# Weight-block sums made in DRAM ahead of time, scan fill redistributed, and operand halves loaded into other tiles, in a hybrid SSM and attention layer

## The chip, the cores and the metric

One Trainium2 chip, one of its cores. The metric is the device time of one execution in microseconds (us); lower is better. Engines: TensorE (PE; PEld is its weight load), VectorE (DVE), ScalarE (ACT), GpSimd (POOL), SyncE (SP). SP and ACT issue plain DMAs, POOL issues DMAs that may add to what lies at their destination.

## The reference

One layer, 512 tokens, width 2048, all in float32:

```python
h = rmsnorm(x, norm_w)
u = h @ w_in
z_ssm, xbc, dt_f, dt_b, q_a, kv_a, z_attn, g_ssm, g_attn = jnp.split(u, cuts, axis=-1)
xbc = jax.nn.silu(dwconv(xbc, conv_w, conv_b))
xs, bm, cm = jnp.split(xbc, ...)          # 32 heads of 64, 4 groups, state 128
y = ssd_scan(forward) + flip(ssd_scan(flipped)) + d_skip * xs       # chunks of 128 tokens
y = rmsnorm(y * silu(z_ssm), by group) * ssm_norm_w
q = rmsnorm(q_a) @ w_uq;  kv = rmsnorm(kv_a) @ w_ukv                # 16 heads, rotary part of 64
o = bidir_attention(q, k, v) * jax.nn.silu(z_attn)
merged = sigmoid(g_ssm) * (y @ w_proj_ssm) + sigmoid(g_attn) * (o @ w_proj_attn)
return rmsnorm(x + merged @ w_out, final_norm_w)
```

## The kernel before

**Arithmetic.** Each float32 operand is split in two parts: `h` is its copy rounded to TensorE's float32r format, made on ScalarE, and `l` the rest, made on VectorE. A product is three matmuls (h·h, h·l, l·h) of 512 columns into PSUM. A weight chunk is 128 x 1024 floats (512 KB): loaded by SP into one of three `wraw` buffers (or into `X` or `Y`, below), split into `wh` and `wl` (three buffers each), and used by 24 matmuls in the projections of the input, 12 in the blocked products.

**Order of work.** TensorE's instructions run in the order in which the program emits them. The other engines' are put in order by a scheduler with priorities: `tc.high_priority(offset=n)` lets an instruction pass n others, and `keep_in_program_order` pins one. Weight loads have an offset of 160 (`LOAD_AHEAD`), splits 60 (`AHEAD`). A tile pool recycles its buffers by tag; a pool that opens over the memory of a closed one waits tile by tile for the last users there.

**Stages.** (1) RMSNorm of x, transposed into `h_h`, `h_l`; the first input columns (`xbc_gen`, group 0); sums of blocks of h for the next stage (`h_sums`); `S3` and `x21` are stored in DRAM. (2) Three gates (`wz`, `wgs`, `wga`), each a 2048 x 2048 weight multiplied by Strassen-Winograd with seven block products per half (`Strassen.pair`, `cp` 0 and 1): P1, P5, P6, P2, P3, P7, P4, each 48 matmuls. Ahead of them S3 is loaded back and split over `x21` in `h_h`/`h_l`; P7 uses it. (3) The bidirectional scan, four groups (`ssd_group`). A group begins with transposes, goes through the states of its chunks (the state phase), and then makes the decay matrices and diagonal parts chunk by chunk (`seg_make`, `diag`: the chunk phase, VectorE's scans). Between these steps `gap()` emits a share of the fill: the generators of the remaining input columns (`xbc`, `qkv`, `za`), 10 tiles of 48 matmuls per group, in 18 gaps of equal share. `y_norm` normalises y, `y_turn` transposes it on TensorE and stores it in `yn_d`. (4) Preparation of attention (`compressed`, rotary tables), with the rest of the fill. (5) Attention, 16 heads: `scores`, `trans`, `pv`, with the heads' own weights as fill, and at its end `wps.head()` (P1 and P2 of both halves of the y projection). (6) The two projections, `wps` (y) and `wpa` (o): `wps.pair(0, True)`, `wps.pair(1, True)` (P5, P6, P3, P7, P4), `wpa.pair(0)`, `wpa.pair(1)` (all seven). (7) The output product, residual and last norm.

**Block sums of weights.** P5 and P6 need sums of weight blocks, P7 another. In `pair`, with the blocks named by row half and column half, `X` is loaded with block (0,0), and POOL's accumulating DMA (`w_more`) adds block (0,1) to it in SBUF; P5 uses X and adds `Y`, block (1,1), to it on VectorE for P6; (1,0) is added for P4. `Y` is used by P3, then `w_more` adds (0,1) to it for P7. `X` and `Y` have four buffers each. `y_ops` and `o_ops` hold the sums of operand blocks: made in DRAM by POOL (`sums`), loaded in halves by `raw_load` into `wraw`, split by `Ops.split` into slots of tag `opb` (five) or `opa`. The hooks of `wps` and `wpa` say behind which product a load (`L`), a split (`C`) or a part of the sums of o (`o_sums`) is emitted.

**Between attention and the projections** the pool `at` closes and `xb` opens on its memory; S1 and S2 of y are loaded and split, S4 is loaded, and `fill.all()` emits what is left of the head.

**PSUM banks** of a product come from a table by the product's name (`SETS`); the transposes of merged results use the banks of the product before the last.

Of the kernel before, what the change touches and what calls it, by code (L numbers as in the profile page):

```python
# [18 lines left out]
P = 128  # L19
# [53 lines left out]
def build(tc, a):  # L73
# [50 lines left out]

    OPS = ("x11", "x12", "x21", "x22", "S1", "S2", "S3", "S4")
# [206 lines left out]
    class Fill:  # L332
# [16 lines left out]
        def run(self, n):  # L349
            while n > 0 and self.q:  # L350
                n -= self.step()
# [108 lines left out]

    def w_more(t, w, cp, kh, cb, m, ahead_=AHEAD):

        with tc.high_priority(offset=ahead_):
            pool.dma_start(t, a[w][cp, kh, cb, m], accum_op=ALU.add)
# [41 lines left out]
    before_ = deque(["P1", "P1"])  # L506

    def turn_bank(i):

        return SETS[before_[0]][i]("turn")  # L510

    def product(name, op, chunk, extra=None, pre=None):

        bs = [b(name) for b in SETS[name]]
# [16 lines left out]
        before_.append(name)  # L531
        before_.popleft()
# [3 lines left out]
    class Strassen:  # L536
# [47 lines left out]
        def pair(self, cp, headed=False):  # L584
            w = self.w
            X, Y = [], []
            if not headed:
                def c1(m):
                    X.append(w_load(w_tile("X"), w, cp, 0, 0, m))
                    return X[m]  # L590

                p1 = evict((yield from product("P1", self.op("x11"), c1, lambda m, raw: w_more(raw, w, cp, 0, 1, m))), "p1")
# [33 lines left out]
            B = yield from product("P3", self.op("S4"), lambda m: Y[m], lambda m, raw: w_more(raw, w, cp, 0, 1, m),  # L626
# [6 lines left out]
            A = yield from product("P7", self.op("S3"), lambda m: Y[m], None, self.pre(2, 2 * cp + 1))  # L633
# [61 lines left out]
    h_ops.load("S3")  # L695
    for q in range(2):
        h_part("S3", 256, q)
# [19 lines left out]
    def h_back():  # L717
        h_ops.raws["x21"] = []
        for q in range(2):
# [5 lines left out]
                                      ("wga", h_ops, 1, gate(AF.Sigmoid, ga_d)))]  # L725
    gates[2].hooks = {(1, "P7"): [h_back, lambda: [h_part("x21", 256, q) for q in range(2)]]}
# [56 lines left out]
    def y_norm(c, g, y):  # L783
# [7 lines left out]
        dve.tensor_scalar_mul(y, y, rsqrt1(s_))  # L791
# [15 lines left out]
    def ssd_group(g):  # L807
# [727 lines left out]
```

## Time and profile before

| | |
|---|---|
| time, median of 3 runs | 2138.2 us (2128.6 to 2139.95) |
| the profiled execution | 2139.41 us, its span 2137.6 us, mean TensorE clock 0.966 |
| TensorE busy | 1982.9 us (93%), 9074 matmuls |
| VectorE, ScalarE, GpSimd busy | 1469.5 us (69%), 953.0 us (45%), 259.0 us (12%) |
| DMA | 349.20 MB, mean 163 GB/s |

```profile
## 2 busy tenths in 40 slices
PE   6989999999998998997999799999984989999998
PEld 5878888888776777786787688888873767877886
DVE  7966677677569679798687566767662878776342
ACT  5444444444535445445445344444442435444232
POOL 0001010100032221331221000000001010000110
PEclk9999999999999999998999899999996999999999
DMA  5457656855635535565444843524559788876332
```

Each digit is a slice of 53 us and the busy share in tenths. The gates lie in slices 3 to 11, the scan in 11 to 22, attention in 24 to 31, the projections in 31 to 37. A row of the lists has line, engine, operation, written tile <- read tiles, shape, count, then busy us, mean ns of one and idle time ahead of it with what ended most of it. A row of waits has the total in us, the number, and the longest. "Idle ... <-" in a timeline row stands in square brackets.

### The profile page before, as it was taken

Reading aid. Unit: us, or ns where it says so; the run is one execution under the profiler, and the core shown is the slowest. Engines: PE = TensorE matmul, PEld = TensorE weight load, DVE = VectorE, ACT = ScalarE, POOL = GpSimd, SP = SyncE. Lnnn points to the kernel's source line nnn. Section 1 sums busy time; section 2 is a strip of 40 time slices with the busy share of each in tenths; the row PEclk is TensorE's granted clock in tenths of the full one; section 3 lists DMA queues with packets and bytes.
Section 4 is the critical chain, followed back from the end, with each engine's and each line's share of the span. In section 5 each row is a group of like instructions: output and inputs, shape, how many; then the busy total and the mean of one; then the engine's idle time right before and its main releaser. Section 6 shows DMA issues by size and latency. Waiting matters only on the chain.

```text
span 2137.6 us, 24587 instructions
## 1 busy us (share of the span) xinstructions
PE 1982.9 (93%) x9074; PEld 1635.5 (77%) x9074; DVE 1469.5 (69%) x1962; ACT 953.0 (45%) x1332; POOL 259.0 (12%) x225
## 2 busy tenths in 40 slices
PE   6989999999998998997999799999984989999998
PEld 5878888888776777786787688888873767877886
DVE  7966677677569679798687566767662878776342
ACT  5444444444535445445445344444442435444232
POOL 0001010100032221331221000000001010000110
PEclk9999999999999999998999899999996999999999
DMA  5457656855635535565444843524559788876332
GB/s 193 144 173 197 180 125 169 206 137 149 192 105 154 162 99 163 167 192 159 127 144 147 226 133 89 138 85 125 131 177 276 217 234 267 231 223 191 102 126 79
DMA packets 162488, 349.20 MB, mean 163 GB/s; under 512 B 14976, under 2 KB 64256, under 8 KB 161792
## 3 DMA queue, kind: packets, MB, share of 16 engines
q1 hardware_dynamic: 110448, 242.52, 35.8%
q0 software_dynamic: 17088, 58.73, 14.4%
q10 hardware_dynamic: 34832, 46.38, 6.0%
q8 instruction: 71, 1.16, 0.2%
q14 instruction: 49, 0.40, 0.1%
HBM read 295.67 MB, written 64.49 MB: 168 GB/s over the span
## 4 chain that ended last, share of the span: by engine, by line
PE 71%; DVE 12%; DMA 8%; issue 5%; ACT 2%; POOL 0%; ACTq 0%; SPq 0%; DVEq 0%; POOLq 0%
PE P L528 9%; PE P L529 9%; PE P L527 9%; PE xbc L166 3%; PE xbc L167 3%; PE xbc L168 3%; PE f L1402 3%; PE f L1403 3%; PE f L1404 3%; DVE sum L942 2%; PE za L166 2%; PE za L168 2%; PE za L167 2%; DVE wl L428 1%; DVE wl L162 1%
## 5 line engine op out<-in xcount | busy, mean ns | idle before, releaser
L428 DVE TENSOR_TENSOR wl<-X,wh 128x1024 fp32r<-128x1024 f32 x152 | 185.2, 1223 | 88.7 <-ACT wh L427 88.3
L162 DVE TENSOR_TENSOR wl<-wraw,wh 128x1024 fp32r<-128x1024 f32 (+2 forms) x148 | 175.1, 1183 | 101.8 <-ACT wh L161 101.8
L161 ACT CAST wh<-wraw 128x1024 fp32r<-128x1024 f32 (+2 forms) x150 | 145.5, 970 | 217.0 <-PE xbc L167 74.3
L427 ACT CAST wh<-X 128x1024 fp32r<-128x1024 f32 x152 | 159.1, 1053 | 176.4 <-PE P L529 131.4
L428 DVE TENSOR_TENSOR wl<-wraw,wh 128x1024 fp32r<-128x1024 f32 x74 | 91.4, 1236 | 107.3 <-ACT wh L427 107.3
L428 DVE TENSOR_TENSOR wl<-Y,wh 128x1024 fp32r<-128x1024 f32 x80 | 98.0, 1224 | 84.8 <-ACT wh L427 84.6
L527 PE MATMUL P<-wh,h_h 128*128 128x512 f32 x384 | 150.7, 393 | 5.4 <-ACT wh L427 5.4
L166 PE MATMUL xbc<-h_h,wh 128*128 128x512 f32 x384 | 152.8, 398 | 0.0
L528 PE MATMUL P<-wl,h_h 128*128 128x512 f32 x384 | 150.7, 393 | 0.5 <-DVE wl L428 0.5
L167 PE MATMUL xbc<-h_l,wh 128*128 128x512 f32 x384 | 150.7, 393 | 0.0
L168 PE MATMUL xbc<-h_h,wl 128*128 128x512 f32 x384 | 150.7, 392 | 0.0
L529 PE MATMUL P<-wh,h_l 128*128 128x512 f32 x384 | 150.4, 392 | 0.0
L427 ACT CAST wh<-wraw 128x1024 fp32r<-128x1024 f32 x74 | 77.9, 1053 | 152.3 <-PE f L1404 70.1
L427 ACT CAST wh<-Y 128x1024 fp32r<-128x1024 f32 x80 | 83.9, 1052 | 109.0 <-PE P L529 83.2
L168 PE MATMUL za<-h_h,wl 128*128 128x512 f32 x256 | 101.8, 397 | 12.8 <-DVE wl L162 12.8
L527 PE MATMUL P<-wh,S 128*128 128x512 f32 x288 | 112.0, 389 | 0.0
L528 PE MATMUL P<-wl,S 128*128 128x512 f32 x288 | 112.0, 389 | 0.0
L529 PE MATMUL P<-wh,S 128*128 128x512 f32 x288 | 112.0, 389 | 0.0
L166 PE MATMUL za<-h_h,wh 128*128 128x512 f32 x256 | 103.3, 404 | 0.0
L167 PE MATMUL za<-h_l,wh 128*128 128x512 f32 x256 | 101.5, 396 | 0.0
L527 PEld LDWEIGHTS P<-wh,h_h 128*128 128x128 f32 x384 | 72.8, 190 | 21.0 <-ACT wh L427 5.8
L942 DVE TENSOR_TENSOR_SCAN sum<-da,scn 128x512 f32<-128x512 f32 x64 | 85.3, 1346 | 0.0
(615 smaller groups left out, 5127.6 us busy)
## 6 DMA issues: line engine op xcount, KB each, us to landing
wraw<-wi SPq DMA_DIRECT2D x102, 512.0 KB, 3.5
da<-da_d SPq DMA_DIRECT2D x64, 256.0 KB, 3.7
wraw<-wo SPq DMA_DIRECT2D x32, 512.0 KB, 3.5
wraw<-wps SPq DMA_DIRECT2D x24, 512.0 KB, 3.9
xbc_d<-xbc ACTq DMA_DIRECT2D x24, 256.0 KB, 2.5
wraw<-wun SPq DMA_DIRECT2D x16, 384.0 KB, 3.0
o_S<-o_x POOLq DMA_DIRECT2D x12, 512.0 KB, 8.3
xt<-x SPq DMA_DIRECT2D x8, 512.0 KB, 7.9
```

Of the source, the lines that this page charges most:

```text
L161: act.copy(h, raw)
L162: (dve if ahead[0] else pool).tensor_sub(l, raw, h.bitcast(F32))
L166: pe.matmul(out, wh, xh, start=start, stop=False)
L167: pe.matmul(out, wh, xl, start=False, stop=False)
L168: pe.matmul(out, wl, xh, start=False, stop=stop)
L427: act.copy(hi_, raw)
L428: dve.tensor_sub(lo_, raw, hi_.bitcast(F32))
L527: pe.matmul(bs[i], xh, wh, start=(j == 0), stop=False)
L528: pe.matmul(bs[i], xh, wl, start=False, stop=False)
L529: pe.matmul(bs[i], xl, wh, start=False, stop=(j == 7))
L942: dve.tensor_tensor_scan(sums[dd], flat(da), mask, 0.0, ALU.add, ALU.mult)
L1402: pe.matmul(acc, mh, wh, start=(start and k == 0), stop=False)
```

## The change

1. `t_d`: eight DRAM tensors hold T1 = (0,0) + (0,1) and T3 = (1,1) + (0,1) for each column half of `wps` and `wpa`. `t_jobs` makes 32 POOL DMAs for each weight: a copy of 512 KB, and two places later the accumulation of the other block. Those of `wps` are issued from the scan's gaps (`in_background`, every second gap), those of `wpa` in attention, four per head, after a POOL multiply that reads the head's row sums (`pace`).
2. `pair` for these two weights: P1 loads its chunks into `wraw`, P5 loads T1 into X, P7 loads T3 into `wraw`; no `w_more`. The gates keep theirs.
3. `gap()`: shares 0.7, 0.7, six of 0.8, ten of 1.25, and what a gap emits too much is taken from the next. Part of the fill is emitted between the steps of attention's preparation.
4. y is scaled by its norm on ScalarE instead of VectorE.
5. S3 is loaded behind P1 of the first gate and split behind its P5.
6. PSUM banks in a fixed rotation of four sets.
7. S1 and S2 of y are loaded into tiles of tag `X`; an unused tile `place` takes the first `opb` slot; S4's load comes after the rest of the head. `o_sums` keep program order.

```diff
+    t_d = {(w, cp, n): scratch(f"{n}_{w}{cp}", 4096) for w in ("wps", "wpa") for cp in range(2) for n in ("T1", "T3")}
...
         def run(self, n):
-            while n > 0 and self.q:
-                n -= self.step()
+            got = 0
+            while n > got and self.q:
+                got += self.step()
+            return got
...
+    def t_load(t, w, cp, name, m):
+        with tc.high_priority(offset=LOAD_AHEAD):
+            nc.sync.dma_start(t, t_d[w, cp, name][:, m * 1024:(m + 1) * 1024])
+        return t
+
+    def t_jobs(w):
...
+                    jobs.append((lambda d=d, cp=cp, kh=kh, cb=cb, m=m: pool.dma_start(d, a[w][cp, kh, cb, m]),
+                                 lambda d=d, cp=cp, m=m: pool.dma_start(d, a[w][cp, 0, 1, m], accum_op=ALU.add)))
+        order = []
+        for i in range(len(jobs) + 2):
+            if i < len(jobs):
+                order.append(jobs[i][0])
+            if i >= 2:
+                order.append(jobs[i - 2][1])
+        return deque(order)
+
+    background = t_jobs("wps")
+
+    def in_background(n=1):
+        for _ in range(n):
+            if background:
+                tc.keep_in_program_order(background.popleft()())
...
-    SETS = {"P1": (mm, mm), "P5": (pb, pb), "P6": (pa, pa), "P2": (mm, pc), "P3": (mm, mm), "P7": (pb, pb),
-            "P4": (mm, pc), "P1b": (pa, pa), "P2b": (mm, mm)}
+    SETS = ((mm, mm), (mm, pc), (pa, pa), (pb, pb))
+    used = deque([0, 0, 3], maxlen=3)
...
+        used.append((used[-1] + 1) % 4)
+        bs = [b(name) for b in SETS[used[-1]]]
...
                 def c1(m):
+                    if made:
+                        return w_load(w_tile("w"), w, cp, 0, 0, m)
...
             def c5(m):
-                if headed:
-                    X.append(w_load(w_tile("X"), w, cp, 0, 0, m))
-                    w_more(X[m], w, cp, 0, 1, m, LOAD_AHEAD)
+                if made:
+                    X.append(t_load(w_tile("X"), w, cp, "T1", m))
                 Y.append(w_load(w_tile("Y"), w, cp, 1, 1, m))
                 return X[m]
+
+            def c7(m):
+                return t_load(w_tile("w"), w, cp, "T3", m) if made else Y[m]
...
-            B = yield from product("P3", self.op("S4"), lambda m: Y[m], lambda m, raw: w_more(raw, w, cp, 0, 1, m),
+            B = yield from product("P3", self.op("S4"), lambda m: Y[m], None if made else lambda m, raw: w_more(raw, w, cp, 0, 1, m),
...
-            A = yield from product("P7", self.op("S3"), lambda m: Y[m], None, self.pre(2, 2 * cp + 1))
+            A = yield from product("P7", self.op("S3"), c7, None, self.pre(2, 2 * cp + 1))
...
-    h_ops.load("S3")
-    for q in range(2):
-        h_part("S3", 256, q)
...
+    gates[0].hooks = {(0, "P1"): [lambda: h_ops.load("S3")],
+                      (0, "P5"): [lambda: [h_part("S3", 256, q) for q in range(2)]]}
...
-        dve.tensor_scalar_mul(y, y, rsqrt1(s_))
+        act.activation(y, y, AF.Copy, scale=rsqrt1(s_))
...
-        left = [(10 * 48, 10 * 48, 9 * 48, 10 * 48)[g], 18]
+        shares = [0.7] * 2 + [0.8] * 6 + [1.25] * 10
+        left = [0, (10 * 48, 10 * 48, 9 * 48, 10 * 48)[g] / sum(shares)]
 
         def gap():
-            n = left[0] // left[1]
-            left[0] -= n
-            left[1] -= 1
-            fill.run(n)
+            if len(shares) % 2:
+                in_background()
+            left[0] += shares.pop(0) * left[1]
+            left[0] -= fill.run(left[0])
...
     compressed(0, 6, rq_d, V_QN, cq_h, cq_l)
+    fill.run(48)
     compressed(6, 4, rkv_d, V_KN, ckv_h, ckv_l)
+    fill.run(36)
...
+    fill.run(36)
     dve.tensor_scalar(ang2, ang, math.pi / 2, None, ALU.add)
...
+    fill.run(48)
...
+    in_background(len(background))
+    background.extend(t_jobs("wpa"))
+    pace = few(1)
...
+        if background and t == 1:
+            pool.tensor_mul(pace, sm_, sm_)
+            in_background(4)
...
-        return lambda: [f() for f in o_half[n]]
+        return lambda: [tc.keep_in_program_order(f()) for f in o_half[n]]
...
             kk = kp_
+            used.extend([0, 0, 3])
             fill.add("head", wps.head())
...
+    xb.tile([P, 2, 8, 256], F32R, tag="opb", bufs=5, name="place")
     for w in ("S1", "S2"):
-        y_ops.load(w)
-        y_ops.split(w, slot(w))
-    L(y_ops, "S4")()
+        y_ops.raws[w] = [cols.tile([P, 1024], F32, tag="X", bufs=4, name="xraw") for q in range(2)]
+        for q in range(2):
+            nc.sync.dma_start(y_ops.raws[w][q], yn_d[w][:, q * 1024:(q + 1) * 1024])
+        C(y_ops, w)()
     fill.all()
+    L(y_ops, "S4")()
...
-                before_[0] = "P5"
                 product_done()
```

More of the change, by code (lines that the diff above doesn't have):

```diff
@@ L459, in w_load @@
         return t
+    def t_load(t, w, cp, name, m):
[3 more added lines that the diff above has]
+    def t_jobs(w):
+        jobs = []
+        for cp in range(2):
+            for name, kh, cb in (("T1", 0, 0), ("T3", 1, 1)):
+                for m in range(4):
+                    d = t_d[w, cp, name][:, m * 1024:(m + 1) * 1024]
+                    i = 2 * len(jobs) // 2
+                    jobs.append((lambda d=d, cp=cp, kh=kh, cb=cb, m=m: pool.dma_start(d, a[w][cp, kh, cb, m]),
[12 more added lines that the diff above has]
+                tc.keep_in_program_order(background.popleft()())
     def w_more(t, w, cp, kh, cb, m, ahead_=AHEAD):
@@ L584, in pair @@
         def pair(self, cp, headed=False):
-            w = self.w
+            w, made = self.w, (self.w, cp, "T1") in t_d
             X, Y = [], []
@@ L588, in c1 @@
                 def c1(m):
+                    if made:
+                        return w_load(w_tile("w"), w, cp, 0, 0, m)
                     X.append(w_load(w_tile("X"), w, cp, 0, 0, m))
                     return X[m]
-                p1 = evict((yield from product("P1", self.op("x11"), c1, lambda m, raw: w_more(raw, w, cp, 0, 1, m))), "p1")
+                p1 = evict((yield from product("P1", self.op("x11"), c1, None if made else
+                                               lambda m, raw: w_more(raw, w, cp, 0, 1, m))), "p1")
                 self.hook(cp, "P1")
```

8 lines of the change are left out of this document (2 added, 6 removed).

## The prediction

> **What bounds the kernel now.** I read the page first, then TensorE's waits, then busy time by stage, then the queues around each long wait.
>
> ```profile
> span 2137.6 us, 24587 instructions
> PE 1982.9 (93%) x9074; PEld 1635.5 (77%) x9074; DVE 1469.5 (69%) x1962; ACT 953.0 (45%) x1332; POOL 259.0 (12%) x225
> ...
> PE 71%; DVE 12%; DMA 8%; issue 5%; ACT 2%; POOL 0%; ACTq 0%; SPq 0%; DVEq 0%; POOLq 0%
> ```
>
> TensorE is busy for 1982.9 of 2137.6 us and holds 71% of the chain that ended last. The edit changes neither the number nor the size of its matmuls in any way that counts, so what can move is the other 154.7 us, and the time that matmuls run slowly after a wait. The waits say where that is:
>
> ```profile
> PE P1b L527 <- ACT wh L427: 29.7, 1, 29.7
> PE turn L797 <- DVE y L791: 28.8, 4, 9.8
> ...
> PE P L527 <- ACT wh L427: 14.7, 6, 5.4
> PE za L168 <- DVE wl L162: 12.8, 1, 12.8
> ...
> PE loc L167 <- DVE xw_l L879: 3.9, 2, 1.9
> ```
>
> One wait of 29.7 us (a weight chunk's split, between attention and the projections), four of 28.8 us together (the scan's normalised y), one of 12.8 (in the preparation of attention). The edit touches the surroundings of all of them. The stages in numbers (columns: window and its length; PE, PEld, DVE, ACT, POOL busy with their counts; TensorE clock; DMA share, GB/s):
>
> ```profile
> 102.00:122.00 20.00, 14.11 (x49) 10.71 (x48) 8.27 (x9) 7.45 (x9) 2.73 (x3) 0.74 0.83 278
> 644.00:692.00 48.00, 38.21 (x182) 31.43 (x180) 47.90 (x64) 26.06 (x31) 10.69 (x7) 0.92 0.52 162
> 592.00:640.00 48.00, 45.32 (x186) 36.41 (x185) 32.05 (x41) 18.19 (x25) 16.38 (x14) 0.93 0.25 81
> 1240.00:1540.00 300.00, 300.00 (x1607) 256.40 (x1606) 202.84 (x405) 130.77 (x261) 8.49 (x11) 1.00 0.40 111
> 1607.00:1656.00 49.00, 17.58 (x61) 13.11 (x60) 14.49 (x13) 14.02 (x15) 7.69 (x8) 0.65 0.99 272
> 1656.40:1785.28 128.88, 117.27 (x480) 92.34 (x481) 106.15 (x110) 58.85 (x60) 11.15 (x13) 0.95 0.83 248
> 1785.28:1951.10 165.82, 160.84 (x730) 131.46 (x728) 127.67 (x139) 73.41 (x82) 12.90 (x15) 1.00 0.76 217
> 1820.05:1830.93 10.88, 10.88 (x50) 9.01 (x48) 8.30 (x10) 4.22 (x4) 0.86 (x1) 1.00 0.55 160
> 1725.02:1738.49 13.47, 13.01 (x49) 10.17 (x49) 12.25 (x12) 5.74 (x6) 0.00 (x0) 0.85 0.68 173
> 879.50:881.50 2.00, 2.00 (x5) 1.29 (x4) 0.76 (x3) 0.95 (x3) 0.00 (x0) 0.50 0.92 266
> ```
>
> The window from 1820.05 is one undisturbed product: 48 matmuls in 10.88 us, 0.227 each. That is my yardstick. From 1725.02 is a product that follows a wait of 4.6 us (row below): 13.47 us at a clock of 0.85, so about 2.5 us are lost to the slow clock after such a wait. Attention (1240 to 1540) runs at 300.00 of 300 us, so nothing can be won there.
>
> **The change part by part.**
>
> **Attention to projections (1607 to 1656).** 60 matmuls lie in this window (12 of the third head product, 48 of the fourth): 13.6 us by the yardstick. It lasts 49, so 35.4 us are lost. Why:
>
> ```profile
> 1614.91 1.99 ACT L427 CAST S__13055<-xraw 128x1024 fp32r<-128x1024 f32 x2 [15.28 <-DMA o_x<-og]
> ```
> ```profile
> 1607.25 0.33 SPq L458 DMA_DIRECT2D X<-wps  x1
> ...
> 1613.00 0.33 SPq L458 DMA_DIRECT2D X<-wps  x1
> ...
> 1617.24 2.59 SPq L438 DMA_DIRECT2D xraw<-yn_S  x3
> 1629.73 13.59 SPq L458 DMA_DIRECT2D wraw<-wps  x5
> ```
>
> ScalarE stands for 15.28 us before the split of S1, because S1's tile lies on attention's og tiles, whose store it waits for. Meanwhile S1's, S2's and S4's halves hold the three wraw buffers, so the load of the head's next chunk goes out at 1629.73; TensorE's 29.7 us end with its split. The edit takes both causes away: a tile called place takes the slot on og, so S1 lies on others, and the halves of S1 and S2 land in X tiles, so that the five chunk loads find wraw free. What is late next: X buffers lie on attention's last tiles too (the X loads went out at 1607.25 and 1613.00, the first just as attention's last product ended), so S2's second half is issued at about 1613.
>
> ```profile
> X<-wps SPq DMA_DIRECT2D x8, 512.0 KB, 6.2
> X<-wps POOLq DMA_DIRECT2D x8, 512.0 KB, 10.5
> ...
> wraw<-wps SPq DMA_DIRECT2D x24, 512.0 KB, 3.9
> ```
>
> It lands 6.2 us later and is split by about 1622; only the product after next needs it. If the chunks' splits pass it, the loss falls from 35.4 to some 6 us: 29 won, which I take, since the chunks are ready first. If ScalarE keeps program order, the first chunk is split at 1624 and then 13.6 us of work follow with 5 of slow clock: 12 won. Ends: 12 and 35.
>
> **Block sums in DRAM.** Removed: 32 accumulating loads by POOL into X and Y. Added: 32 DRAM copies and 32 DRAM accumulations of 512 KB on POOL's queue (half in the scan, half in heads 0 to 7), and 24 loads on SP (8 for wps, 16 for wpa). In the projections an X chunk costs 6.2 + 10.5 us one after the other today; a ready sum costs one load. The ten wps products take 128.88 us, 20.1 over the yardstick's 108.8; the fourteen of wpa 165.82, at most 13 over 152.3. Of the 20.1, the start of the second wps column is the X chain alone: 4.6 us of wait
>
> ```profile
> 1725.02 0.80 PE L527 MATMUL P<-wh,S__13055 128*128 128x512 f32 x1 [4.62 <-ACT wh L427]
> ```
>
> and 2.6 in the product after it. I take these 7 and 4 more, because the queues get lighter:
>
> ```profile
> q1 hardware_dynamic: 110448, 242.52, 35.8%
> q0 software_dynamic: 17088, 58.73, 14.4%
> ```
>
> Per MB, q0 took 5.2 us of all engines' time, q1 3.2. The projections lose 32 x 0.52 MB x 5.2 = 88 us of it and gain 24 x 0.52 x 3.2 = 40. So 11 won; ends: 20, and minus 20 where the 24 new loads crowd the three wraw buffers (rivals).
> In attention 88 us of DMA time go into 8 of the 16 heads, half of its 300 us and more, on top of a share of 0.40: about 0.95 with 20 us a head. TensorE ran full at 0.83 and more in places, with loads ahead; I charge 2 us, ends 0 and 16 (2 per head). POOL's little multiply waits for a head's sums; behind it only its own issues queue. In the scan the same 88 us spread over four groups (share 0.5 to about 0.65): free, unless the issues hold POOL:
>
> ```profile
> L1229 POOL DMA_DIRECT2D yn_S<-yn_x x4 | 4.4, 1214 | 50.2 <-DMA yn_x<-y 43.7 <-DMA yn_S<-yn_S 6.5
> L1226 POOL DMA_DIRECT2D yn_S<-yn_x x2 | 1.1, 559 | 2.8 <-issue 1.6 <-DMA yn_x<-y 1.1
> ```
>
> 16 copies x 0.56 + 16 accumulations x 1.21 = 28 us on a POOL that works 16.38 of 48 us (state phase) and 10.69 of 48 (chunk phase): hidden; 2 us charged for G2 and xw waiting their turn. An accumulation comes two places behind its copy, several gaps later; it finds it landed.
>
> [...]
>
> ```profile
> L952 DVE TENSOR_TENSOR G<-G,G 128x512 f32<-128x512 f32 x32 | 29.3, 914 | 2.8 <-POOL G L951 2.8
> ...
> L953 DVE TENSOR_TENSOR G<-G,E 128x512 f32<-128x512 f32 x32 | 21.8, 681 | 0.7
> ```
>
> The same shape costs 681 or 914 ns on VectorE. If every issue held VectorE for its length, the 28 us would be the scan's price (a rival).
>
> **Scan's fill.** Per group 480 matmuls in 18 gaps of 27; now two of 18, six of 20.5, ten of 32. In the chunk phase (644 to 692) VectorE is full (47.90 of 48) and TensorE waits for y; in the state phase (592 to 640) VectorE has 32.05. Five chunk gaps precede the first wait: 5 x 5.4 matmuls bring TensorE there 6.1 us later; VectorE gets 27/24 x 1.2 = 1.4 us of splits more (a split serves 24 matmuls) and loses one y scaling, which goes to ScalarE (45% busy):
>
> ```profile
> L428 DVE TENSOR_TENSOR wl<-wraw,wh 128x1024 fp32r<-128x1024 f32 x74 | 91.4, 1236 | 107.3 <-ACT wh L427 107.3
> ...
> L791 DVE TENSOR_SCALAR y<-y,rr 128x512 f32<-128x512 f32 x16 | 8.5, 530 | 0.3
> ```
>
> Net 5.3 us less for each of the four waits (7.2 on average): 21 won, and some 4 of slow clock. Against it, the two first gaps shrink by 8.7 matmuls, 2.0 us each; today waits of up to 1.9 us stand behind them (loc), so I charge 3 us per group, 12. The state loop keeps 4.7 us gaps over a chain of about four short passes and has shown no wait: 2 charged. With POOL's 2: 25 - 16 = 9 won. Ends: 35 (waits and slow clock gone, no price) and minus 25 (waits unchanged; 2 us lost in two gaps of each group, 16, and 9 of the issues' 28).
> [...]
>
> ```profile
> 878.84 1.68 PE L326 MATMUL rp<-sq_q,cst 128*128 128x512 f32 x2 [2.09 <-DVE y L966]
> ```
>
> **S3 out of the way of the first gate product (102 to 122).** 48 matmuls need 10.9 of these 20 us: 9.1 lost.
>
> ```profile
> 103.67 1.06 ACT L427 CAST h_h<-xraw 128x1024 fp32r<-128x1024 f32 x1 [0.67 <-PE xbc L168]
> ```
> ```profile
> 95.09 11.25 SPq L458 DMA_DIRECT2D wraw<-wz  x3
> 106.39 2.36 SPq L458 DMA_DIRECT2D X<-wz  x4
> ```
>
> S3's halves hold wraw; SP stands at a wraw load till 106.34, and the X loads that the first product needs go out behind it. Moved behind two products, S3's two loads and 2 x (1.05 + 1.2) us of splits lie beside TensorE-bound gates (4.5 us if uncovered). 6 won; ends 0 and 9.
>
> **Preparation of attention.** The wait of 12.8 us plus 2.5 of slow clock: a chunk's second split stands on VectorE behind a key tile whose load took
>
> ```profile
> 1194.15 13.11 DMA raw<-qkv_d
> ```
>
> Fill is now taken in between, so the splits come ahead of these tiles. 10 won; ends 0 and 15, since the sums of y still load the queues then.
>
> **Bank order, o_sums in program order:** a bank comes again after four products instead of three or more, each 10.88 us: no wait now, none then. 0.
>
> **Sum:** 29 + 11 - 2 + 9 + 6 + 10 = 63 us, off the profiled execution's 2139.4: 2076. (The median, 2138.2, is 1.2 lower; within 0.5%, 11 us, is about what a measurement can't tell from no change.)
>
> **Rivals.**
> *ScalarE keeps program order at the transition.* 12 instead of 29: 2093. For it: that is how it stood at 1614.91. Against: the chunks' operands are there earlier.
> *The scan loses.* Short first gaps and 28 us of issues that hold VectorE: minus 25 instead of 9: 2110. For it: VectorE at 47.90 of 48 and the 914 ns. Against: issues beside the gates' splits today cost nothing visible.
> *Slower: three wraw buffers.* P7 (four times) and wpa's P1 (twice) now stream through wraw, where operand halves also wait to be split. With one buffer left, a chunk takes 3.9 + 1.05 + 1.2 = 6.2 us against 2.7: 14 us per product, six products, 84: 2160. It decides once it strikes five of the six (70 over 63). Against: the product at 1820.05 streams through wraw at full speed.
> *The waits only move.* ScalarE or DMA is late a little further on; only half the gates and the transition's sure 12 stay, minus the charges: about 2130.
>
> **How the numbers follow.** Forecast 0.52 (own range 2055 to 2095); transition in order 0.17; scan loses 0.13; waits only move 0.08; wraw crowds 0.06; better than forecast (scan and projections near their ends, about 2040) 0.04. Faster by over 0.5%: 0.52 + 0.17 + 0.13 + 0.04 and a sliver of the fourth: 0.87; same 0.07, slower 0.06. The range 2042 to 2115 leaves out the last two losing cases and the best.
>
> **What would show it.** Right: the P1b wait of 29.7 gone from TensorE's list and 1607 to P5 in about 20 us; the turn waits under 10 us in sum; no 12.8 us wait on za; the first gate product waiting under 2 us; wps products within 11 us of the yardstick; POOL issues without DVE passes growing. Wrong: ScalarE idle on a half of S1 or S2 with a wraw split behind it, long waits on P7 or P1 for wraw, waits on loc or off in the state phase, attention below 99% busy.

## The result, and the profile after it

The changed kernel takes 2117.4 us in the median (2111.1 to 2127.4), the kernel before, run beside it, 2139.1: a ratio of 0.990 [0.988, 0.993]. That is 22 us won where 63 were forecast, and outside the range, 2 us above its upper end. Medians further down leave out two executions that were far slower than the others of their kernel (2530 and 5086 us). The profiled execution took 2111.87 us, 27.5 less than the profiled execution of before, and it is this difference that I divide up. The page of the changed kernel:

```profile
PE 1979.2 (94%) x9074; PEld 1633.7 (77%) x9074; DVE 1467.0 (70%) x1946; ACT 958.6 (45%) x1344; POOL 275.1 (13%) x265
...
PE 75%; DVE 10%; DMA 6%; issue 5%; ACT 2%; POOL 1%; SPq 0%; ACTq 0%; DVEq 0%; POOLq 0%
```

TensorE's waits in it (us in total, times, longest):

```profile
PE P L561 <- ACT wh L431: 44.4, 9, 13.5
...
PE turn L834 <- ACT y L828: 12.1, 4, 4.2
...
PE loc L169 <- DVE xw_l L917: 7.6, 5, 2.4
...
PE za L170 <- DVE wl L164: 5.0, 1, 5.0
```

The head's 29.7 us are gone, the y waits have fallen from 28.8 to 12.1 us and the preparation's from 12.8 to 5.0. But the waits of the products for a chunk's split have tripled, from 14.7 us to 44.4 (9.1 of these stand ahead of wps's first product, what is left of the head's 29.7). The stages say where those are (the same windows as before, moved along with the work; the columns are those of the prediction). First of before, for the two that the prediction gave in another cut, then of after:

```profile
583.10:1233.30 650.20, 588.21 (x2679) 484.52 (x2680) 495.61 (x694) 306.91 (x452) 152.60 (x109) 0.94 0.51 155
...
1263.20:1571.80 308.60, 301.49 (x1572) 254.34 (x1570) 216.06 (x436) 140.85 (x280) 9.63 (x12) 0.99 0.43 118
```
```profile
102.00:122.00 20.00, 14.12 (x52) 10.80 (x51) 8.80 (x9) 7.46 (x8) 2.78 (x3) 0.83 0.82 278
...
583.50:1203.00 619.50, 583.63 (x2688) 480.58 (x2689) 491.03 (x674) 311.55 (x463) 172.88 (x141) 0.97 0.65 190
...
1233.10:1545.90 312.80, 302.18 (x1571) 254.39 (x1570) 215.88 (x436) 140.87 (x280) 32.52 (x51) 0.99 0.64 168
...
1581.30:1604.00 22.70, 13.63 (x62) 10.95 (x60) 11.46 (x13) 9.26 (x10) 2.84 (x3) 0.86 0.97 333
1604.00:1738.00 134.00, 118.29 (x480) 93.80 (x480) 109.48 (x112) 62.62 (x63) 1.70 (x2) 0.93 0.84 278
1738.00:1925.50 187.50, 167.36 (x728) 135.43 (x729) 127.86 (x137) 72.76 (x81) 0.00 (x0) 0.94 0.54 180
```

| stage | before | after | difference | forecast |
|---|---|---|---|---|
| first gate product (window 102 to 122) | clock 0.74, PE 14.11 of 20 | clock 0.83, PE 14.12 of 20 | 0 | -6 |
| scan and preparation | 650.2 | 619.5 | -30.7 | -19 |
| attention up to its last head | 308.6 | 312.8 | +4.2 | +2 |
| to the first projection product P5 | 49.2 | 22.7 | -26.5 | -29 |
| ten products of wps | 128.9 | 134.0 | +5.1 | -11 (both) |
| fourteen of wpa | 165.8 | 187.5 | +21.7 | |
| the rest | | | -1.3 | 0 |

The sum of the differences is -27.5. The transition came as forecast, the scan better; the projections went 27 us the wrong way, 38 from where I had put them. This is how a wpa product looked there, on ScalarE and on SyncE's queue:

```profile
1877.61 2.00 ACT L431 CAST m<-xraw 128x1024 fp32r<-128x1024 f32 x2
1889.41 1.04 ACT L431 CAST wh<-wraw 128x1024 fp32r<-128x1024 f32 x1 [9.79 <-DMA wraw<-T_wpa]
1895.57 1.04 ACT L431 CAST wh<-wraw 128x1024 fp32r<-128x1024 f32 x1 [5.11 <-DMA wraw<-T_wpa]
```
```profile
1854.07 6.12 SPq L442 DMA_DIRECT2D xraw<-m_d  x3
...
1882.12 0.32 SPq L442 DMA_DIRECT2D xraw<-m_d  x1
...
1883.86 20.52 SPq L467 DMA_DIRECT2D wraw<-T_wpa  x4
```

The chunks come 6.2 us apart, where one is needed every 2.7. wraw is a ring: three buffers, used in turn by all tiles of that tag, the halves (xraw) among them. From 1854.07 three halves of the merged tensor's blocks 0 and 1 were loaded and held all three buffers; block 0's were cast from 1877.61 on, so no T3 chunk could be loaded ahead, and the first went out at 1883.86. From then on the halves of block 1 hold two of the three (the second was issued at 1882.12) until their split behind P7; each T3 chunk goes through the third: load, cast, subtraction, next load. That is the chain of 3.9 + 1.05 + 1.2 us that the prediction priced in its slower rival, "three wraw buffers", and gave 6 in 100.

### The profile page after: what moved, and what is told of

Same layout as the page of the kernel before. It is cut to its first block, busy times and chain, and to the rows that moved or that the text cites. A ratio compares the mean times of both kernels' runs of the same rounds, so it can differ in the third digit from the quotient of the medians.

```text
span 2110.1 us, 24659 instructions
## 1 busy us (share of the span) xinstructions
PE 1979.2 (94%) x9074; PEld 1633.7 (77%) x9074; DVE 1467.0 (70%) x1946; ACT 958.6 (45%) x1344; POOL 275.1 (13%) x265
## 4 chain that ended last, share of the span: by engine, by line
PE 75%; DVE 10%; DMA 6%; issue 5%; ACT 2%; POOL 1%; SPq 0%; ACTq 0%; DVEq 0%; POOLq 0%
PE P L562 11%; PE P L563 11%; PE P L561 11%; PE f L1456 3%; PE f L1454 3%; PE f L1455 3%; PE za L170 2%; PE za L168 2%; PE za L169 2%; PE xbc L168 2%; PE xbc L170 2%; PE xbc L169 2%; DVE sum L980 2%; DVE wl L164 1%; PE pb L1249 1%
## 5 line engine op out<-in xcount | busy, mean ns | idle before, releaser
L432 DVE TENSOR_TENSOR wl<-X,wh 128x1024 fp32r<-128x1024 f32 x144 | 175.5, 1222 | 86.5 <-ACT wh L431 85.9
L431 ACT CAST wh<-X 128x1024 fp32r<-128x1024 f32 x144 | 151.4, 1054 | 162.6 <-PE P L563 145.2
L432 DVE TENSOR_TENSOR wl<-wraw,wh 128x1024 fp32r<-128x1024 f32 x98 | 120.6, 1231 | 148.1 <-ACT wh L431 146.3
L431 ACT CAST wh<-wraw 128x1024 fp32r<-128x1024 f32 x98 | 103.2, 1053 | 203.7 <-PE f L1456 74.9
L432 DVE TENSOR_TENSOR wl<-Y,wh 128x1024 fp32r<-128x1024 f32 x64 | 78.3, 1223 | 64.2 <-ACT wh L431 64.1
L431 ACT CAST wh<-Y 128x1024 fp32r<-128x1024 f32 x64 | 67.4, 1054 | 91.2 <-PE P L563 83.3
L170 PEld LDWEIGHTS xbc<-h_h,wl 128*128 128x128 f32 x384 | 72.5, 189 | 16.3 <-DVE small L827 0.8
```

What stands on the lines that cost most here:

```text
L170: pe.matmul(out, wl, xh, start=False, stop=stop)
L431: act.copy(hi_, raw)
L432: dve.tensor_sub(lo_, raw, hi_.bitcast(F32))
```

## The experiments

The theory to be tested: the loss in the projections is the crowded ring wraw. Its rival: the ready sums' loads themselves are slow, because the DMA engines are full (a share of 0.84 in wps); then another ring helps nothing. The runs were made in four sets: the first four below; the next four; halves in X and Y, S3 pinned, the sums made twice, and the first two of these together; the convolution held, all sums in attention, and these two together. The kernel before, beside which each ratio was taken, took 2141.0, 2138.4, 2134.0 and 2138.8 us in them. A difference of a few us between runs of two sets therefore says little by itself, and there I go by the traces.

**T3 through another ring.** Sums T3 are loaded into the four Y tiles, which P3 has just left:

```diff
             def c7(m):
-                return t_load(w_tile("w"), w, cp, "T3", m) if made else Y[m]
+                return t_load(w_tile("Y"), w, cp, "T3", m) if made else Y[m]
```

> The changed kernel with one edit: P7's T3 chunks are loaded into Y tiles instead of wraw. Theory A (three wraw buffers are crowded by operand halves that wait for their splits): the waits ahead of P7 go, in wps (16.8 - 10.9, 14.3 - 10.9, 14.8 - 10.9, 14.8 - 10.9 us) and in wpa's second P7 (36.1 us from its turn to its end, 11.7 needed): 30 to 42 us less than the changed kernel, about 2080. Theory B (the T loads themselves are slow, being strided rows of a DRAM tensor, or the DMA queues are full): the same waits in another buffer, 2112 or more.

Measured: 2078.4 us, ratio 0.970 [0.967, 0.973]. One word is worth 39 us. The same bytes go by the same queue, so it was not the DMA engines.

**P1's chunks too**, into X tiles:

```diff
                 def c1(m):
                     if made:
-                        return w_load(w_tile("w"), w, cp, 0, 0, m)
+                        return w_load(w_tile("X"), w, cp, 0, 0, m)
```

> As e1_t3_in_y, and P1's chunks of wpa go into X tiles as in the kernel before, so that no product but those that did so before streams through wraw. Theory A: also the wait of 4.2 us ahead of wpa's first P1 and the 3.5 us in it go: 7 us less than e1, about 2072, with all products of the projections within 10 us of 24 x 10.9 us. Theory B: as e1.

Measured: 2070.2 us, ratio 0.966 [0.962, 0.969]. The two projections of this kernel:

```profile
1611.70:1725.90 114.20, 113.14 (x481) 91.87 (x482) 104.94 (x107) 60.65 (x62) 1.70 (x2) 0.97 0.88 297
1725.90:1885.90 160.00, 159.43 (x730) 131.62 (x728) 129.03 (x140) 73.48 (x82) 0.00 (x0) 1.00 0.67 228
```

294.7 us before, 321.5 in the changed kernel, 274.2 here: with the ring free, the ready sums win 20, the upper end that the prediction gave for this term. TensorE is busy for 113.1 of 114.2 and 159.4 of 160.0 us.

**The halves later, the ring unchanged.** Block 1's halves are loaded after P7 instead of before it; T3 stays in wraw:

```diff
-        (1, "P3"): [m_split(0), m_load(1)], (1, "P7"): [m_split(1)]})
+        (1, "P3"): [m_split(0)], (1, "P7"): [m_load(1)], (1, "P4"): [m_split(1)]})
```

> The changed kernel with T3 still in wraw, but in wpa's second column the halves of merged block 1 are loaded behind P7 and split behind P4, one product later than in the changed kernel. Theory A: the two halves no longer hold two of three wraw buffers during that P7; its chunks, now 6.2 us apart, run at 2.7, and about 20 us go (2097), unless the output product then waits for block 1 (at most 10 back). Theory B: T chunks stay 5 us and more apart, 2115.

Measured: 2100.2 us, ratio 0.980 [0.977, 0.984]: 17 us of the loss gone without touching a chunk's load. The ring is relieved from its other side, and the cause is shown from both. Of the 25 us that this P7 lost, the wait of 13.5 ahead of it is gone; the product itself still takes 20.1 us, because block 0's halves hold two buffers until their split, as before.

**The transition's edits alone**, in the kernel before, without ready sums:

```diff
+    xb.tile([P, 2, 8, 256], F32R, tag="opb", bufs=5, name="place")
     for w in ("S1", "S2"):
-        y_ops.load(w)
-        y_ops.split(w, slot(w))
-    L(y_ops, "S4")()
+        y_ops.raws[w] = [cols.tile([P, 1024], F32, tag="X", bufs=4, name="xraw") for q in range(2)]
+        for q in range(2):
+            nc.sync.dma_start(y_ops.raws[w][q], yn_d[w][:, q * 1024:(q + 1) * 1024])
+        C(y_ops, w)()
     fill.all()
+    L(y_ops, "S4")()
```

> The kernel before with the transition's edit alone (tile place, halves of S1 and S2 in X tiles, S4's load behind the rest of the head). If that edit stands by itself: 26 us less than before, 2113. If it needs the block sums (X must first be free of the halves, then takes its load and POOL's accumulation, 6.2 + 10.5 us): TensorE waits for X at P5 and only 10 to 15 us are left, 2125.

Measured: 2136.0 us, ratio 0.997 [0.995, 1.000]. TensorE's wait for the chunk has only changed its name; on ScalarE:

```profile
1645.98 1.04 ACT L427 CAST wh<-X 128x1024 fp32r<-128x1024 f32 x1 [22.14 <-DMA X<-wps]
```

And on GpSimd:

```profile
1636.14 1.14 POOL L1229 DMA_DIRECT2D o_S<-o_x  x1 [7.98 <-DMA o_S<-o_S]
1636.85 4.04 POOL L464 DMA_DIRECT2D X<-wps  x4
```

The halves sit in X until they are split, so the first X chunk is loaded at 1619.74; it landed 6.6 us later. GpSimd issued the accumulation only at 1636.85, behind two sums of o that waited for DMAs, some 10 us after that landing, and it took 9.0 us more. So the 26.5 us of the transition belong to the ready sums and the freed ring together; I had given them to the ring and the place tile alone. How much of the sums' part is the accumulation itself and how much its place behind the sums of o, no run separates.

**The scan's gap shares alone**, in the kernel before:

```diff
-        left = [(10 * 48, 10 * 48, 9 * 48, 10 * 48)[g], 18]
+        shares = [0.7] * 2 + [0.8] * 6 + [1.25] * 10
+        left = [0, (10 * 48, 10 * 48, 9 * 48, 10 * 48)[g] / sum(shares)]
```

> The kernel before with one part of the change, the scan's uneven gap shares (and the accounting that lets a gap give back what an oversized step took). The changed kernel's scan and preparation (from the turn of dt to the rotary products) took 30.7 us less than before, where 19 were forecast. Theory A, the shares carry it: fill left out of the state phase shortens each of its four stretches by 8 to 13 us and lengthens the chunk phases by less; the four turn waits fall from 28.8 us to about 15. 2138 minus 18 to 22: 2118. Theory B, the shares are a wash (the short first gaps pay for the rest, as the prediction's charges of 12 and 2 us had it) and the y scaling on ScalarE carries it: 2130 to 2140, turn waits above 20 us.

Measured: 2111.5 us, ratio 0.988 [0.986, 0.990]. **The preparation's fill alone:**

```diff
     compressed(0, 6, rq_d, V_QN, cq_h, cq_l)
+    fill.run(48)
     compressed(6, 4, rkv_d, V_KN, ckv_h, ckv_l)
+    fill.run(36)
...
+    fill.run(36)
     dve.tensor_scalar(ang2, ang, math.pi / 2, None, ALU.add)
...
     act.activation(cosT, ang2, AF.Sin)
+    fill.run(48)
```

> The kernel before with one part of the change, the four stretches of fill between the preparation's tiles. Forecast: 10 us won, by the 12.8 us wait on za's second split gone; the changed kernel still has 5.0 us of it. Theory A: 6 to 10 us less, 2130. Theory B: the fill taken early is missing at the end of the preparation, the wait moves to the rotary products or to the first fetched heads, and the time stays within 3 us of 2138.

Measured: 2130.8 us, ratio 0.997 [0.995, 0.998]. **The scaling of y alone:**

```diff
-        dve.tensor_scalar_mul(y, y, rsqrt1(s_))
+        act.activation(y, y, AF.Copy, scale=rsqrt1(s_))
```

> The kernel before with one instruction moved, the scaling of y from VectorE to ScalarE, 16 times 530 ns. Theory A, the shares carry the scan: the turn waits fall by 2 us each at most, 2138 minus 2 to 6: 2134. Theory B, the scaling carries it (VectorE was 47.90 of 48 us busy where TensorE waits for y): the turn waits fall from 28.8 to about 15 us and the time to 2120.

Measured: 2131.2 us, ratio 0.997 [0.995, 0.998]. The waits that go with each, first of the shares, then of the fill, then of the scaling:

```profile
PE turn L799 <- DVE y L793: 12.3, 4, 4.3
...
PE loc L167 <- DVE xw_l L880: 7.8, 4, 2.4
```
```profile
PE za L168 <- DVE wl L162: 5.1, 1, 5.1
```
```profile
PE turn L797 <- ACT y L791: 28.4, 4, 9.3
```

The shares carry the scan: 16.5 us of y waits go and 3.9 come at loc, and the stretch from the turn of dt to the rotary products shrinks from 650.2 to 626.6 us. The scaling leaves the y waits where they were (28.4) and still wins 7 us: VectorE's busy time from the turn of dt to the rotary products falls from 495.6 to 487.4 us, and that stretch from 650.2 to 641.3; I had counted it as a help to the y waits. The fill is worth 7.5 where I said 10.

**The halves ahead of the Y loads**, in the second run's kernel:

```diff
+        with tc.high_priority(offset=LOAD_AHEAD):
-        y_ops.raws[w] = [cols.tile([P, 1024], F32, tag="X", bufs=4, name="xraw") for q in range(2)]
+            y_ops.raws[w] = [cols.tile([P, 1024], F32, tag="X", bufs=4, name="xraw") for q in range(2)]
...
```

> The changed kernel with sums T3 streamed through Y tiles and P1's chunks through X tiles (2070.2 us measured), and the loads of the halves of S1 and S2 given the priority that weight loads have, so that they go out ahead of the four Y loads on SyncE's queue instead of behind them. Theory A: what is left of the transition (9.3 us of TensorE waiting for a chunk's split that stands behind S1's and S2's on ScalarE) is the lateness of these halves; they land 4 to 6 us earlier and the time falls to 2065. Theory B: the X tiles they land in become free only with attention's last product, whatever the order of the queue, and the first chunk now lands later behind them: the wait stays at 8 us or grows, 2070 to 2074.

Measured: 2072.5 us, ratio 0.970 [0.968, 0.972], no gain. ScalarE:

```profile
1596.02 2.00 ACT L431 CAST S__13136<-xraw 128x1024 fp32r<-128x1024 f32 x2 [4.60 <-DMA o_x<-og]
...
1606.32 1.04 ACT L431 CAST wh<-X 128x1024 fp32r<-128x1024 f32 x1 [5.46 <-DMA X<-T_wps]
```

The loads go out earlier, but S1's split now waits for attention's last store (og again): it begins 11.2 us after that stage's last product, where it began 12.2 us after it. (The next expectation's "5 us earlier" counts 4 us by which this run stood earlier as a whole.) The X tile comes free behind it, and the first T1 chunk is issued at 1598.35 and cast 8 us later.

**Halves in two X and two Y tiles**, on top of that:

```diff
-            y_ops.raws[w] = [cols.tile([P, 1024], F32, tag="X", bufs=4, name="xraw") for q in range(2)]
+            y_ops.raws[w] = [cols.tile([P, 1024], F32, tag="X" if w == "S1" else "Y", bufs=4, name="xraw") for q in range(2)]
```

> As the run with the loads of the halves of S1 and S2 ahead of the Y loads (2072.5 us measured: the halves' splits came 5 us earlier, but the first sums T1 could be loaded only when these had left the four X tiles, 8 us before the first chunk's split), and S1's halves in two X tiles, S2's in two Y tiles. Theory A, the tiles are the wait: two T1 chunks and two Y chunks load beside the halves, the 9.0 us wait falls to 1 to 3 us: 2064. Theory B: ScalarE waits for S1's place, which attention's store of its last tile (10 us) sets free, and the first chunk's split stands behind it anyway: the wait falls by 3 us at most, 2069.

Measured: 2069.0 us, ratio 0.969 [0.966, 0.972], beside 2070.2 no gain that can be told. The windows up to P5 and of wps:

```profile
1579.80:1596.40 16.60, 13.63 (x61) 10.96 (x60) 7.95 (x8) 9.06 (x11) 1.71 (x2) 1.00 0.97 323
1596.40:1718.50 122.10, 114.45 (x481) 92.63 (x482) 107.76 (x111) 60.57 (x62) 2.83 (x3) 0.96 0.87 294
```

The transition falls from 22.8 to 16.6 us, and wps grows from 114.2 to 122.1. Its third product stands 4.6 us for a split on VectorE, which is behind sums that wait for chunks in wraw:

```profile
1631.20 1.23 DVE L648 TENSOR_TENSOR X<-X,wraw 128x1024 f32<-128x1024 f32 x1 [1.42 <-DMA wraw<-wps]
1632.34 2.35 DVE L432 TENSOR_TENSOR wl<-Y,wh 128x1024 fp32r<-128x1024 f32 x2
```
```profile
1605.84 2.02 SPq L442 DMA_DIRECT2D xraw<-yn_S  x3
...
1615.50 7.00 SPq L462 DMA_DIRECT2D wraw<-wps  x4
```

The wait has only moved. It is the ring again, in part: from 1605.84 three halves of S4 and S3 hold all of wraw, and SyncE's load of the first chunk waits for their splits till 1615.50. The DMA engines are nearly full there as well (a share of 0.97 up to P5, 0.87 in wps); how much each of the two costs, no run here separates.

**S3's splits pinned** behind the first gate product's chunks. In the changed kernel they stood on ScalarE at the same place as before, for all that the program wrote them later; so the forecast's step had not been made at all:

```diff
+    def s3_back():
+        for q in range(2):
+            h, l = part_of(1, 0, q)
+            raw = view4(h_ops.raws["S3"][q])
+            tc.keep_in_program_order(act.copy(h, raw))
+            dve.tensor_sub(l, raw, h.bitcast(F32))
...
-                      (0, "P5"): [lambda: [h_part("S3", 256, q) for q in range(2)]]}
+                      (0, "P5"): [s3_back]}
```

> The changed kernel with sums T3 streamed through Y tiles and P1's chunks through X tiles (2070.2 us measured), and S3's two splits held in the order in which they are written, behind the first gate product's chunks, on ScalarE. In the changed kernel they stood ahead of them in spite of the move. Theory A: the 5.4 us wait at the first gate product is S3's, as the prediction had it; it goes, with its slow clock, 6 to 9 us: 2062 to 2064. Theory B: the wait is the X loads' own lateness behind the load queue, or S3's halves now hold two of three wraw buffers while the first product streams through the third (6.2 us a chunk): nothing won or 8 us lost, 2070 to 2078.

Measured: 2066.4 us, ratio 0.968 [0.965, 0.970]. The wait at the first gate product is still 5.42 us. SyncE's queue and ScalarE now read:

```profile
95.39 7.41 SPq L462 DMA_DIRECT2D X<-wz  x4
```
```profile
109.04 0.78 ACT L387 ACTIVATE cacc<-xbc,vec 128x512 f32<-128x512 f32 x1 [7.06 <-PE xbc L170]
112.26 0.63 ACT L391 ACTIVATE xbc<-cacc 128x512 f32<-128x512 f32 x1 [2.45 <-DVE cacc L390]
...
113.32 2.94 ACT L431 CAST wh<-X 128x1024 fp32r<-128x1024 f32 x3 [0.43 <-ACT xbc L391]
```

S3 is out of the way and the chunk loads leave 11 us earlier, and still the first chunk is cast at 113.32. ScalarE stood idle for 7.06 us, for a convolution that needs the last xbc product, and for 2.45 more between its two passes; the casts are behind it in its order, with their data there.

**The convolution held** until the second chunk's split is written (on top of the last kernel):

```diff
+        if g == 0 and i == 3:
+            held.append(lambda: put(xbc_d[g][i], conv_silu(p_, 3, st("xbc"), st)))
+            return
...
             h, l = w_split(raw)
+            if held and m == 1:
+                held.pop()()
```

> As the run with S3's splits pinned (2066.4 us measured; the 5.42 us wait at the first gate product stayed, with S3 gone from in front of it and the chunk loads 10 us earlier), and the convolution behind the last product before the gates written after the second chunk's split instead of ahead of the first. Theory A: the first chunk was held by ScalarE's order alone, by the convolution's two passes with three of VectorE between them (109.0 to 112.9); the wait of 5.4 us and the slow clock behind it (18 matmuls at half speed, 4 us) go: 2057 to 2060. Theory B: the product waits for something else (its banks, the weight tiles of the chunk before): the wait stays above 4 us and the time at 2064 to 2068.

Measured: 2058.4 us, ratio 0.962 [0.960, 0.964]. The window of the forecast:

```profile
102.00:122.00 20.00, 20.00 (x90) 16.55 (x89) 11.94 (x12) 9.55 (x11) 3.63 (x4) 1.00 1.03 283
```

20.00 of 20 us at full clock: with the loads already early, the wait and its slow clock go, 8 us of time (the turn of dt comes 9.0 us earlier in the trace, at 573.7 against 582.7). It takes both edits. In the changed kernel the first X chunk was issued at 106.30 and landed 6.5 us later, 0.5 us before its cast at 113.30; by these rows the convolution moved alone could win about that half us, an estimate, for no run holds it without S3 pinned.

**The sums made twice**, the second time into DRAM that nothing reads (on top of the second run's kernel; spare holds the same jobs for other tensors):

```diff
             if background:
                 tc.keep_in_program_order(background.popleft()())
+            if spare:
+                tc.keep_in_program_order(spare.popleft()())
```

> The changed kernel with sums T3 streamed through Y tiles and P1's chunks through X tiles (2070.2 us measured), in which GpSimd issues every copy and every accumulation of the block sums a second time, into DRAM that nothing reads: the price of making the sums, doubled. Theory A, the forecast's charges: 2 us in the scan and 2 in attention: 2074. Theory B: the three parts of the change in scan and preparation won 27, 7 and 7 us alone, 41, but the changed kernel only 31, so that the sums cost 10 there, and attention 4: 2084.

Measured: 2084.3 us, ratio 0.975 [0.972, 0.978], 14 more by the times, some 20 by the ratios. From the turn of dt to the rotary products, and attention:

```profile
584.40:1218.60 634.20, 586.85 (x2689) 480.29 (x2690) 488.29 (x674) 311.65 (x463) 194.53 (x173) 0.96 0.74 211
1252.80:1565.80 313.00, 302.45 (x1571) 255.18 (x1570) 216.05 (x436) 141.07 (x280) 55.21 (x83) 0.98 0.81 222
```

The scan pays 11 us (623.1 with the sums made once, the longest of nine traces with the same scan); attention, at 313.0, as much as with them made once (312.8 in the changed kernel), though its DMA share is 0.81 over the whole.

**All sums in attention, none in the scan** (on top of S3 pinned):

```diff
-    background = t_jobs("wps")
+    background = deque()
...
-    in_background(len(background))
+    background.extend(t_jobs("wps"))
     background.extend(t_jobs("wpa"))
...
-            in_background(4)
+            in_background(8)
```

> As the run with S3's splits pinned (2066.4 us), and all block sums made in attention's heads 0 to 7, eight issues a head, none in the scan. Theory A: the sums cost 10 us in the scan and nothing in attention (made twice they lengthened the way from the turn of dt to the rotary products by 11 us, attention by none): 2056. Theory B, the forecast's price of 2 us in the scan, and DMA full in attention costs a few: 2064 to 2072.

Measured: 2067.1 us, ratio 0.966 [0.964, 0.967], no change. Without and with the sums in the scan (this kernel, and the one with S3 pinned):

```profile
584.10:1201.40 617.30, 584.50 (x2689) 481.91 (x2690) 489.87 (x674) 313.25 (x464) 154.97 (x109) 0.97 0.53 163
```
```profile
582.70:1204.00 621.30, 585.57 (x2689) 480.84 (x2690) 491.10 (x674) 311.61 (x463) 173.30 (x141) 0.97 0.65 189
```

These two differ by 4.0 us, but that is no price: the nine traces with one set of sums in the scan took 615.7 to 623.1 us for this stretch, 619.6 in the mean, and the two without took 617.3 and (in the last run below) 622.0, 619.6 in the mean. What the first set costs the scan is too small to be told here, and the forecast's 2 is neither borne out nor refuted; a second set costs 11 at least. So making the sums doesn't explain why shares, fill and scaling won 41 us alone and the change 31 there, and I can't place these 10 (the parts shorten the same stretches, so that gains need not add, but no run here shows how they overlap).

**Together.** Halves in X and Y with S3 pinned:

> The halves of S1 and S2 in X and Y tiles and S3's splits pinned, together, with sums T3 in Y tiles and P1's chunks in X tiles. If both gains hold and add up: 2056 to 2058. If neither holds: 2070 to 2078.

Measured: 2073.4 us (2063.9 to 2073.7), ratio 0.969 [0.965, 0.973]: no gain that can be told from the second run's 2070.2. Convolution held with all sums in attention:

> The last two edits together. If both gains hold and add up: 2047 to 2050; if one of them: 2056 to 2060; if none: 2066.

Measured: 2057.8 us, ratio 0.961 [0.960, 0.963], the same as the convolution held alone. The best version is that one: T3 in Y, P1 in X, S3 pinned, convolution held, 2058 us, some 80 less than before and 60 less than the change as it was made.

## Why the prediction was wrong, step by step

- **Block sums and projections (+11 forecast, -27 measured): the step that failed.** I took 20 to -20 as its ends and chose 11 by the weight of the queues; the other end, "where the 24 new loads crowd the three wraw buffers", I made a rival with 6 in 100. It struck four of its six products. TensorE's waits at them (ended at, length) and the products' own lengths beyond 10.88 us:

| product | wait | product longer by |
|---|---|---|
| wps, first P7 (1646.2) | 5.0 | 3.4 |
| wps, second P7 (1707.9) | 3.8 | 4.0 |
| wpa, first P1 (1738.0) | 4.2 | 3.5 |
| wpa, second P7 (1890.5) | 13.5 | 11.6 |

  That makes 49 us, against the 20 that the ready sums win with the ring free: 29 lost by this count, 27 by the stages, more than the 20 I had set as the worst end. The price of 6.2 us a chunk was exact in the fourth of them; the rival's count of buffers was not. Three of the four paid 8 us and not 14, and two nothing; the fourth paid 25, because ahead of it the halves held all three buffers and not two. That the losses in the projections stayed at 49 us and not 84 is why the change still came out faster. What I held against it was one product of before that streamed through wraw at full speed. At 1820 no operand half lay in the ring; the row shows the ring free, not how it does when shared. The place to look was which halves are loaded ahead of P7 and P1, by the hooks in the code, and how long they stay.
- **S3 (6 forecast, 0 measured).** Two errors. The edit's place in the program was taken for its place on ScalarE; the splits stayed where they were. And of the two rows that I quoted for the cause, S3's cast at 103.67 ended 8.7 us before the first chunk's cast began (113.40); what lay directly ahead of that cast was the convolution, and I didn't read that far. The other row, the load queue that stood behind S3's halves, was right: it kept the first chunk from landing until just before that cast. Two holds ended together, and taking away S3's alone won nothing.
- **Transition (29 forecast, 26.5 measured): right in size.** Og and the ring were the causes named, and "what is late next" was right as to the X tiles, but not as to who waits: P5's own first chunk, T1, was loaded only at 1596.81, once S1's split had freed an X tile, and 9.1 us of wait remain. And the run with the edits alone won 6: without ready sums the X chain takes their place. The credit belonged in part to the sums.
- **Scan (9 forecast) and preparation (10): 31 measured.** Direction right, size low: I charged 12 us for the short first gaps; the wait at loc grew by 3.7 us in all. The shares alone won 27, where I had 25 less the charges. No run shows the 4 us of slow clock in those 25 by itself; over this stretch the granted clock was 0.94 before and 0.97 after.
- **Attention (-2 forecast, -4.2 measured).** The twelve traces with sums in attention took 2 to 7 us longer there than the six without, which agree within 0.5; sums made twice, or all made there, cost it nothing more. Why a second set is free, no run shows.
- **Bank order and o_sums (0 forecast).** No run has either alone; what the stages above leave over is -1.3 us.
- **Issues on GpSimd.** 32 issues in the scan took 23.1 us, where 28 were forecast:

```profile
L479 POOL DMA_DIRECT2D T_wps<-wps x16 | 13.4, 836 | 0.0
L478 POOL DMA_DIRECT2D T_wps<-wps x16 | 9.7, 605 | 0.0
```

  Neither form is stretched, as a rule, beside a busy VectorE: two accumulations beside an idle VectorE took 817 and 842 ns, eleven beside one that worked throughout 798 to 891; two copies 564 and 585, against 543 to 567 in nine cases and some 800 in three. Nor is VectorE held by the issues, as the rival "the scan loses" had it: in the changed kernel's scan and preparation, a weight split took 1.22 us in the median with nothing on GpSimd beside it (68 of them), 1.21 to 1.23 beside an issue alone (6), and 1.69 in the median (1.21 to 2.06) beside GpSimd's products (12). The 914 ns that the prediction quoted are a mean of 23 cases of some 680 ns and nine of 1.46 to 1.53 us, and each of the nine lies beside a GpSimd product for 0.9 to 1.0 us: the next one, for the one whose result it reads ended up to 1.0 us before it began. So it is GpSimd's products that VectorE's work slows beside, by these rows and not each time, and not its issues. Most of VectorE's work beside these issues is TENSOR_TENSOR and scans, so other operations are hardly tried by them.

## What to carry to other kernels

When an edit sends a stream through a ring of buffers, list who else holds buffers of that ring at that moment and for how long; a row in which the stream ran at full speed counts only if the same tenants were there. A wait's cause is what stands directly ahead of the late instruction on its own engine, with its input already there, not an earlier instruction that also took time. Two things can hold it till the same moment; then taking away either one shows nothing, and both have to go. And before a move is priced, see whether the order on the engine changes at all: a scheduler that places work by readiness may put it back.

## What the runs showed of the hardware

TensorE's clock stood at half speed behind one wait of about 2 us and at full speed behind another. These windows of the changed kernel follow waits of 2.10 us (ended at 702.46), 2.15 (1005.46) and 5.42 (114.40):

```profile
114.40:116.40 2.00, 1.54 (x3) 0.93 (x4) 2.00 (x2) 1.91 (x2) 0.48 (x1) 0.50 0.62 225
...
704.40:706.40 2.00, 2.00 (x6) 1.60 (x6) 2.00 (x4) 0.97 (x3) 0.00 (x0) 0.50 0.93 270
...
1007.50:1009.50 2.00, 2.00 (x11) 1.65 (x10) 0.41 (x1) 1.64 (x3) 0.00 (x0) 1.00 1.03 322
```

Behind the 5.42 us wait come 5 us at half speed (114.40 to 119.40), and the product takes 13.9 us instead of 10.88, 3.0 on top of the wait; of the two waits of about 2.1 us one is followed by a window at 0.50 and one isn't. The length of the wait alone doesn't tell these two apart. Twelve small matmuls (128 or 64 columns) follow the first and precede the second, but that doesn't tell them apart either: in the kernel before, twelve of the same shapes precede the wait of 2.09 us that ended at 878.84, as they do the second here, and the window from 879.50, in the prediction's stage table, stands at 0.50. What does decide, no run here shows.
